# MLP in fp16 pieces: transfers in the order of the source, and what moves with them

## The chip, the cores and the metric

The kernel runs on one core of a Trainium2 chip. The metric is the device time of one execution in microseconds (us). Five engines work side by side, each through its own queue in order: TensorE (PE, matmuls and transposes), VectorE (DVE), ScalarE (ACT), GpSimd (POOL) and SyncE (SP), which here only issues transfers. A transfer is issued by SP, and lands some us later; the waits of SP's queue hold everything that is issued behind them.

## The reference, cut to what matters

One layer of an encoder on 1024 rows of width 1024 in float32: attention, an output projection with a residual, an MLP of width 4096 with a residual, and a last norm. The change touches the second norm and the MLP.

```python
def rms_norm(x, g):
    y = xf * lax.rsqrt(jnp.mean(xf * xf, axis=-1, keepdims=True) + EPS)
    return (y * g.astype(jnp.float32)).astype(x.dtype)
...
        h = h + jnp.einsum('bsm,md->bsd', y, w_out[layer])
        n2 = rms_norm(h, norm2_g[layer])
        u = jnp.square(jax.nn.relu(jnp.einsum('bsd,df->bsf', n2, w_ff1[layer])))
        h = h + jnp.einsum('bsf,fd->bsd', u, w_ff2[layer])
    return rms_norm(h, final_norm_g)
```

## The kernel before

**Pieces.** The MLP computes float32 products in float16: each operand is scaled by a power of two, taken from the largest magnitude in it, and split into a high and a low half; `mm3` makes three matmuls of it (high x high, high x low, low x high). `split` makes the halves: ACT writes the high one (L1357), and DVE (L1361) or POOL (L1359) the low one. A 2 x 2 block product is made of seven products of sums of blocks instead of eight; a product is 24 matmuls of 128 x 512. Its number p says which sums it takes, and the products of a group come in the order 1, 5, 6, 3, 7, 2, 4 (the last group of phase 2 in another).

**Phase 1** makes u from the normed rows: eight groups n, one for each 512 columns of w_ff1, with seven products each; "(n, p)" is one of them. Its weight tiles are w1 (four to a group), their sums T and their halves W; PE adds into PSUM tiles f1. Between products the maximum over each result is kept (topf), ACT takes relu and square, and after p = 4 DVE adds the pieces (k and v tiles, L1421 to L1427). The seven results of a group are stored to DRAM as ud, one transfer each (`put`, L1440).

**Phase 2** makes the output from u and w_ff2: four groups g of two parts n, seven products p for each part, first both parts of one p, then of the next: V0_1, V1_1, V0_5, V1_5 and so on. Its u tiles are loaded from ud one product's operand at a time (`load2u`, L1492), its weights w2 eight tiles to a group (`load2w`, L1498); U and V are the halves of both and Z the sums of weights. PE adds into f2 tiles (chains a, b and c, two banks each); when both parts of a product are through, DVE adds the bank to the output's accumulators C (`add_up`, L1637), which frees the bank for a later product. The operands of a product are made two products ahead (`prepare2`).

**Scales.** A scale needs the maximum over all partitions. `see` takes the maximum of a tile (tops), `gather` (L1163) that of its columns (top), and then it has to reach all partitions. In phase 1, and for the first group of phase 2, PE transposes it (`spread`, all_w and all_u). In phase 2 it goes through DRAM: `write` (L1170) stores top, `read` (L1174) loads it back to all partitions. Then `bits` (L1178) reduces it to topall and a few operations on single columns make the scale (up, uup) and what undoes it (down, udown). A row of n2 is multiplied by xup, a power of two from the gain's maximum, beside its rstd (L1219).

**What sets the order.** Each engine's instructions are put in a fixed order ahead of time by a planner that estimates when operands and buffers will be there; the loop over products gives it the work, and a manual dependency can force an order (the class `InOrder` chains what is issued through it, as the source has it). Before, SP's transfers are left to that planner.

## Time and profile before

| | us |
|---|---|
| three runs, median (lowest to highest) | 1085.91 (1085.35 to 1087.11) |
| the profiled execution | 1085.46 |
| its span | 1083.7 |
| PE busy | 1013.8 |
| DVE busy | 790.1 |
| ACT busy | 652.2 |
| POOL busy | 402.2 |

The span counts from the first to the last instruction. The mean granted clock of PE over it is 0.975. A busy time counts an engine's instructions, not its waits; the list of waits adds an engine's idle time up by what ended it, as total, number of times and longest one. In the groups of instructions, and in the timeline, numbers of buffers are left out (w2_4_00 is w), and the name is what is written, then what is read. A timeline row has the start, the length, the engine, the line and the operation, and in brackets the idle time before it.

### The profile page before, as it was taken

The page shows a single profiled execution, that of the slowest core. Times are in us where ns is not written, and L with a number is a line of the kernel's source. Part 1 is how long each engine was busy: PE and PEld are TensorE (multiplying, and loading weights), DVE is VectorE, ACT ScalarE, POOL GpSimd, SP SyncE. Part 2 cuts the span into 40 slices and gives each one's busy share as a digit, 9 for nine tenths or more (in the row PEclk, how much of TensorE's full clock was granted, in tenths as well). Part 3 has the DMA queues.
Part 4 walks back from the last instruction along what each step waited for, and adds up shares of the span by engine and source line. Part 5 has one row for each costly group of instructions (what it writes and reads, how often), then busy time and mean ns, then how long its engine had stood idle before and what let it go on. Part 6 is the DMA issues. An engine that isn't in the chain of part 4 may idle for free.

```text
span 1083.7 us, 13981 instructions
## 1 busy us (share of the span) xinstructions
PE 1013.8 (94%) x4815; PEld 594.1 (55%) x4815; DVE 790.1 (73%) x1299; ACT 652.2 (60%) x1033; POOL 402.2 (37%) x327
## 2 busy tenths in 40 slices
PE   9999999999979999899899899899898899799997
PEld 7888877777656777444344344344343344244443
DVE  6477787867667377978556566569988699588886
ACT  8676767666767656865466376368364444365446
POOL 0467674254434723041534434343131023035113
PEclk9999999999989999999999999999899899899999
DMA  9943628999999933133434344278897254251004
GB/s 361 249 130 97 165 78 192 201 214 218 242 216 250 279 139 135 59 117 139 153 119 174 136 143 167 98 268 309 260 333 271 80 175 155 80 194 39 1 1 155
DMA packets 142726, 184.04 MB, mean 170 GB/s; under 512 B 78656, under 2 KB 96576, under 8 KB 142656
## 3 DMA queue, kind: packets, MB, share of 16 engines
q1 hardware_dynamic: 142512, 182.89, 56.7%
q8 instruction: 38, 0.62, 0.3%
q14 instruction: 32, 0.26, 0.1%
q10 hardware_dynamic: 144, 0.26, 0.1%
HBM read 103.43 MB, written 42.99 MB: 135 GB/s over the span
## 4 chain that ended last, share of the span: by engine, by line
PE 28%; DVE 19%; DMA 9%; ACT 9%; issue 6%; POOL 2%; SPq 0%; DVEq 0%; ACTq 0%; POOLq 0%
PE f L169 9%; PE f_a L169 6%; DMA w<-in_w_ff_dram 4%; PE op_A L169 4%; DVE tops_w L1158 3%; PE f_c L169 3%; DVE V L1361 3%; ACT w L1324 2%; PE op_B L169 2%; PE f_b L169 2%; DVE C L1637 2%; DMA u<-ud 2%; DVE T L1331 2%; DVE Z L1331 1%; DMA top<-top_w 1%
## 5 line engine op out<-in xcount | busy, mean ns | idle before, releaser
L169 PE MATMUL f<-X,W 128*128 128x512 f16 x1344 | 299.3, 385 | 3.5 <-POOL W L1359 2.8
L169 PEld LDWEIGHTS <-U 128*128 128x128 f16 x1356 | 133.8, 99 | 191.2 <-issue 28.1
L169 PEld LDWEIGHTS <-W 128*128 128x128 f16 x1344 | 133.0, 99 | 166.0 <-issue 9.8
L169 PE MATMUL f_a<-V,U 128*128 128x512 f16 x756 | 171.6, 388 | 18.6 <-DVE C L1637 13.6
L1359 POOL TENSOR_TENSOR U<-u,U 128x1024 f16<-128x1024 f32 x32 | 76.9, 2411 | 237.8 <-ACT U L1357 216.4
L1359 POOL TENSOR_TENSOR W<-T,W 128x1024 f16<-128x1024 f32 x29 | 65.4, 2266 | 104.3 <-ACT W L1357 99.7
L1158 DVE TENSOR_REDUCE tops_w<-w 128x1 f32<-128x1024 f32 x64 | 76.2, 1213 | 33.6 <-DMA w<-in_w_ff_dram 33.6
L169 PE MATMUL f_c<-V,U 128*128 128x512 f16 x384 | 85.9, 384 | 5.4 <-DVE up L1140 4.2
L1359 POOL TENSOR_TENSOR W<-w,W 128x1024 f16<-128x1024 f32 x23 | 54.0, 2347 | 93.3 <-ACT W L1357 63.6
L1355 ACT ACTIVATE u<-u,uup 128x1024 f32<-128x1024 f32 x32 | 36.4, 1143 | 64.5 <-DMA u<-ud 64.4
L169 PE MATMUL op_A<-w_o,y 128*128 128x512 f32 x192 | 58.2, 431 | 8.1 <-DVE ts_vB L430 5.2
L617 ACT ACTIVATE P_B<-P_B,nm_B 128x640 f32<-128x640 f32 (+2 forms) x64 | 44.2, 690 | 29.6 <-DVE nm_B L614 14.4
L862 DVE SCALAR_TENSOR_TENSOR H_B<-P_B,rc_B,H_B 128x640 f16<-128x640 f32 (+2 forms) x64 | 51.0, 825 | 10.4 <-ACT H_B L857 10.0
L169 PE MATMUL ip_qB<-nT,w_qB 128*128 128x512 f32 x192 | 53.8, 406 | 1.1 <-DVE t_kB L404 1.0
L1403 ACT ACTIVATE k<-f 128x1024 f32<-128x1024 f32 x24 | 24.4, 1018 | 49.6 <-PE f L169 49.5
L1413 DVE CUSTOM_DVE_ANT_0 k<-f,k 128x1024 f32<-128x1024 f32 x24 | 29.2, 1219 | 34.4 <-PE f L169 34.2
L169 PE MATMUL ip_kB<-nT,w_kB 128*128 128x512 f32 x192 | 53.7, 405 | 0.0
L1414 ACT ACTIVATE k<-k,down 128x1024 f32<-128x1024 f32 x24 | 27.4, 1142 | 41.1 <-DVE topf L1413 41.0
L1357 ACT ACTIVATE V<-Z,up 128x1024 f16<-128x1024 f32 x32 | 36.5, 1140 | 25.3 <-DVE Z L1331 22.9
L169 PE MATMUL ip_vB<-nT,w_vB 128*128 128x512 f32 x192 | 51.2, 400 | 0.0
L1357 ACT ACTIVATE U<-u,uup 128x1024 f16<-128x1024 f32 x24 | 27.4, 1141 | 38.8 <-DMA u<-ud 15.5
L169 PE MATMUL ip_qA<-nT,w_qA 128*128 128x512 f32 x192 | 50.2, 395 | 0.3 <-DVE VA L175 0.3
(273 smaller groups left out, 2035.5 us busy)
## 6 DMA issues: line engine op xcount, KB each, us to landing
w<-in_w_ff_dram SPq DMA_DIRECT2D x64, 512.0 KB, 5.8
u<-ud SPq DMA_DIRECT2D x56, 512.0 KB, 5.3
ud<-k SPq DMA_DIRECT2D x48, 512.0 KB, 2.6
KkB<-t_kB SPq DMA_DIRECT2D x32, 256.0 KB, 5.1
xr<-in_x_dram SPq DMA_DIRECT2D x8, 512.0 KB, 8.6
st_o<-in_w_out_dram SPq DMA_DIRECT2D x8, 512.0 KB, 4.9
h<-in_x_dram SPq DMA_DIRECT2D x8, 512.0 KB, 4.8
hB<-h SPq DMA_DIRECT2D x8, 512.0 KB, 2.6
```

Of the source, the lines that this page charges most:

```text
L169: pe(nc.tensor.matmul(*args, **kw))
L617: nc.scalar.activation(pr, pr, AF.Exp, bias=nm, scale=-1.0, accum_out=sm)
L862: nc.vector.scalar_tensor_tensor(lo, q, rc, hi, ALU.mult, ALU.subtract)
L1158: nc.vector.tensor_reduce(self.column(), flat(src), mybir.AxisListType.X, ALU.max, apply_absolute_value=True)
L1331: engine.tensor_tensor(t, a, b, op)
L1355: nc.scalar.activation(full, full, AF.Copy, scale=up)
L1357: nc.scalar.activation(w[0], full, AF.Copy, scale=1.0 if up is None else up)
L1359: engine.tensor_tensor(w[1], full, w[0], ALU.subtract)
L1361: engine.scalar_tensor_tensor(w[1], full, up, w[0], ALU.mult, ALU.subtract)
L1403: nc.scalar.activation(kept[p], ps, AF.Copy)
L1413: dve.tensor_tensor_reduce(v, ps, v, 1.0, 0.0, ALU.add, ALU.max, top)
L1414: nc.scalar.activation(v, v, AF.Relu, scale=down1[n])
```

## The change

- **Transfers in the source's order.** From the start of the MLP's loop all its transfers go through `InOrder`, so that SP issues them as the program's loops have them.
- **Stores one product later.** `put` only notes a store; the notes are issued when the next product has been written. What is left after group 7 is issued at the end of phase 1, ahead of phase 2's loop.
- **u scales.** The transpose of a pair of groups' u maximum comes at (n, 3) instead of (n, 5).
- **Weights.** All four w1 tiles come from the same pool of pages. The w2 tiles of the next group are loaded two at a time at four steps, and their maxima are taken three steps after the load. top is written at step 8 instead of 9 and still read at step 10. The last u scale is written, read and made at steps 1, 3 and 6 instead of 1, 2 and 5, and the last C is loaded at step 9 instead of 5.
- **u in staging tiles.** u tiles go in turn to two small pools of three tiles each instead of to pages, and are loaded four products ahead instead of three.
- **Rows.** The power of two goes into the scale and the epsilon of the norm's own rstd (`rstd` with `scale` and `eps`), and the eight multiplications of r by xup go.

```diff
@@
-    def rstd(ss, n, width, name, r=None, then=None):
+    def rstd(ss, n, width, name, r=None, then=None, scale=None, eps=None):
...
-        nc.scalar.activation(u, ss, AF.Sqrt, bias=eps4, scale=1.0 / (4 * n))
+        scale = 1.0 / (4 * n) if scale is None else scale
+        nc.scalar.activation(u, ss, AF.Sqrt, bias=eps4 if eps is None else eps, scale=scale)
...
-        r = rstd(ss, D, 1, f"n2_{tb}")
-        nc.vector.tensor_tensor(r, r, xup, ALU.mult)
+        r = rstd(ss, D, 1, f"n2_{tb}", scale=xscale, eps=xeps)
@@
-                w1s[n, kh, j] = (page1 if j or (n, kh) == (1, 1) else stage)([P, 4, 2 * P], f"w1_{n}_{kh}{j}")
-                load(w1s[n, kh, j], src.rearrange("(k p) c -> p k c", p=P))
+                w1s[n, kh, j] = page1([P, 4, 2 * P], f"w1_{n}_{kh}{j}")
+                queue[0].dma_start(w1s[n, kh, j], src.rearrange("(k p) c -> p k c", p=P))
@@
+        while stores:
+            stores.pop(0)()
         kept = saved.setdefault(n, {})
@@
     def put(n, p, v):
-        nc.sync.dma_start(flat(ud[n][p - 1]), v)
+        stores.append(lambda: queue[0].dma_start(flat(ud[n][p - 1]), v))
@@
     def load2u(n, p):
-        u2s[n, p] = page([P, 2, HALF], f"u{n}_{p}", F32)
-        nc.sync.dma_start(u2s[n, p], ud[n][p - 1])
+        if len(u2s_made) % 2 == 0 or len(u2s_made) == 1:
+            u2s[n, p] = stage([P, 2, HALF], f"u{n}_{p}")
+        else:
+            u2s[n, p] = main.tile([P, 2, HALF], F32, tag="tst", bufs=TST, name=f"u{n}_{p}")
+        u2s_made.append((n, p))
+        queue[0].dma_start(u2s[n, p], ud[n][p - 1])
@@
+    queue[0] = InOrder(nc.sync)
     for at, (n, p) in enumerate(order1):
...
-        if p == 5 and n and n % GQ == 0:
+        if p == 3 and n and n % GQ == 0:
             scale_of_u(n // GQ - 1)
...
+    while stores:
+        stores.pop(0)()
     mp_.close()
@@
         if g + 1 < NQ // GQ:
-            if step in range(8):
-                load2w(*blocks2(g + 1)[step])
-            if step in range(2, 10):
-                see2(g + 1, blocks2(g + 1)[step - 2 :][:1])
-            if step in (9, 10):
-                (top2[g + 1].write if step == 9 else top2[g + 1].read)()
+            loads = (0, 1, 2, 3) if g else (1, 2, 4, 5)
+            if step in loads:
+                for tile2 in blocks2(g + 1)[2 * loads.index(step) :][:2]:
+                    load2w(*tile2)
+            if step - 3 in loads:
+                see2(g + 1, blocks2(g + 1)[2 * loads.index(step - 3) :][:2])
+            if step in (8, 10):
+                (top2[g + 1].write if step == 8 else top2[g + 1].read)()
@@
-        if g == 0 and step in (1, 2, 5):
+        if g == 0 and step in (1, 3, 6):
...
-        if at in (0, 1, 3, 5):
-            load_acc(*into[{0: 1, 1: 5, 3: 6, 5: 4}[at]])
+        if at in (0, 1, 3, 9):
+            load_acc(*into[{0: 1, 1: 5, 3: 6, 9: 4}[at]])
```

The planner's fixed orders move with it. Line numbers of the changed kernel are 3 to 19 higher here, and what goes through `InOrder` shows that class's line (L150). Three places follow; a row has the line, the operation, what it writes and reads, and the shape, and the last number of a name is the buffer's.

**DVE at group 7 of phase 1**, about the scale of w2's first group (tops_w2_0, top_w2_0, topall_w2_0). The ISA rows are the addition with a maximum at the end of product (7, 3). Before:

```order
L1158 TENSOR_REDUCE tops_w2_0_6854<-w2_1_10_6822 128x1
L1423 TENSOR_TENSOR v6_6761<-k6_1_6538,v6_6761 128x1024
L1331 TENSOR_TENSOR T7_4_6946<-w1_7_10_6504,T7_6_6784 128x1024
L1163 TENSOR_REDUCE top_w2_0_6894<-tops_w2_0_6854 128x1
L1425 TENSOR_TENSOR k6_1_6538<-k6_5_6568,k6_1_6538 128x1024
L1427 TENSOR_TENSOR k6_6_6610<-k6_6_6610,k6_1_6538 128x1024
L1413 ISA k7_6_6888,topf_7_6929<-f1_7_5_6827,k7_6_6888 128x1024
L1413 ISA topf_7_6929 128x1
L1178 TENSOR_REDUCE topall_w2_0_6936<-all_w2_0_6934 128x1
```

and now:

```order
L1161 TENSOR_REDUCE tops_w2_0_6849<-w2_1_00_6811 128x1
L1161 TENSOR_REDUCE tops_w2_0_6849<-w2_1_01_6813 128x1
L1161 TENSOR_REDUCE tops_w2_0_6849<-w2_1_11_6815 128x1
L1419 ISA k7_6_6883,topf_7_6924<-f1_7_5_6822,k7_6_6883 128x1024
L1419 ISA topf_7_6924 128x1
L1161 TENSOR_REDUCE tops_w2_0_6849<-w2_1_10_6817 128x1
L1166 TENSOR_REDUCE top_w2_0_6889<-tops_w2_0_6849 128x1
L1181 TENSOR_REDUCE topall_w2_0_6930<-all_w2_0_6928 128x1
```

The pass over (7, 3) now stands ahead of the last tile's maximum and of top_w2_0; before, it stood behind both. On PE the transpose that reads top_w2_0 stands right behind (7, 3) both times.

**SP at the boundary of the phases.** ud7 are the stores of group 7, u0 and u1 loads of phase 2, C the accumulators. Before:

```order
L1440 DMA ud6_3_152<-k6_6_6610 128x1024
L1492 DMA u1_5_7071<-ud1_5_119 128x1024
L1498 DMA w2_2_00_7073<-in_w_ff2_dram 128x2x512
L1605 DMA C000_7083<-hB0_88 128x2x512
L1605 DMA C001_7085<-hB1_89 128x2x512
L1492 DMA u0_6_7115<-ud0_6_113 128x1024
L1498 DMA w2_2_01_7117<-in_w_ff2_dram 128x2x512
L1440 DMA ud7_2_158<-k7_6_6888 128x1024
L1605 DMA C110_7128<-hB2_90 128x2x512
L1605 DMA C111_7130<-hB3_91 128x2x512
```

and now:

```order
L150 DMA u0_5_6895<-ud0_5_112 128x1024
L150 DMA ud7_2_158<-k7_6_6883 128x1024
L150 DMA ud7_4_160<-k7_5_6847 128x1024
L150 DMA ud7_1_157<-k7_1_6809 128x1024
L150 DMA ud7_5_161<-k7_5_6847 128x1024
L150 DMA ud7_7_163<-v7_7041 128x1024
L150 DMA ud7_6_162<-k7_1_6809 128x1024
L150 DMA ud7_3_159<-k7_6_6883 128x1024
L150 DMA u1_5_7066<-ud1_5_119 128x1024
L150 DMA u0_6_7068<-ud0_6_113 128x1024
L150 DMA C000_7078<-hB0_88 128x2x512
L150 DMA C001_7080<-hB1_89 128x2x512
```

The store of k7_6 after its last addition (ud7_3) is now ahead of u1_5 and of all that phase 2 loads after it; before, u1_5 and the first C were issued ahead of every store of group 7.

**DVE in phase 2**, about the scale that comes back from DRAM (topall_w2_2; scales of group 2). Before, late in group 0:

```order
L1637 SCALAR_TENSOR_TENSOR C000_7083<-f2_0_b_0_7491,down2_0_6943,C000_7083 128x1024
L1163 TENSOR_REDUCE top_w2_2_7974<-tops_w2_2_7712 128x1
L1637 SCALAR_TENSOR_TENSOR C001_7085<-f2_0_b_1_7492,down2_0_6943,C001_7085 128x1024
L1331 TENSOR_TENSOR Z3_5_7674<-w2_3_01_7279,w2_3_00_7243 128x1024
L1361 SCALAR_TENSOR_TENSOR U3_5_7676<-u3_5_7632,uup_1_6035,U3_5_7676 128x1024
L1178 TENSOR_REDUCE topall_w2_2_8088<-all_w2_2_8012 128x1
L1331 TENSOR_TENSOR Z2_6_7714<-w2_2_11_7160,Z2_5_7636 128x1024
L1133 TENSOR_SCALAR topall_w2_2_8088<-topall_w2_2_8088 128x1
L1361 SCALAR_TENSOR_TENSOR V3_5_7679<-Z3_5_7674,up2_1_7561,V3_5_7679 128x1024
```

and now, in the middle of group 1:

```order
L1652 SCALAR_TENSOR_TENSOR C111_7127<-f2_1_c_1_7724,down2_1_7560,C111_7127 128x1024
L1365 SCALAR_TENSOR_TENSOR U2_7_7872<-u2_7_7792,uup_1_6099,U2_7_7872 128x1024
L1365 SCALAR_TENSOR_TENSOR V2_7_7875<-Z2_7_7870,up2_1_7558,V2_7_7875 128x1024
L1335 TENSOR_TENSOR Z3_7_7904<-w2_3_11_7277,w2_3_01_7239 128x1024
L1365 SCALAR_TENSOR_TENSOR U3_7_7906<-u3_7_7827,uup_1_6099,U3_7_7906 128x1024
L1652 SCALAR_TENSOR_TENSOR C010_7205<-f2_1_a_0_7643,down2_1_7560,C010_7205 128x1024
L1181 TENSOR_REDUCE topall_w2_2_8085<-all_w2_2_8009 128x1
L1365 SCALAR_TENSOR_TENSOR V3_7_7909<-Z3_7_7904,up2_1_7558,V3_7_7909 128x1024
L1652 SCALAR_TENSOR_TENSOR C011_7207<-f2_1_a_1_7644,down2_1_7560,C011_7207 128x1024
```

Before, it stood ahead of the splits of V3_5, the second p of group 1, and of C100, the last addition of group 0; now it stands behind the addition of f2_1_a, which holds product V3_6.

More of the change, by code (lines that the diff above doesn't have):

```diff
@@ L38 @@
 AHEAD2 = 2
-LOAD2 = 3
+LOAD2 = 4
 LOOK_AHEAD = 2
@@ L51 @@
 V_UP = 13
-PAD = 88
+PAD = 80
 X_UP, W_UP, U_UP = 7, 12, 11
@@ L183, in rstd @@
         q = small.tile([P, width], F32, tag=f"rq{width}", bufs=2, name=f"q_{name}")
-        nc.scalar.activation(u, ss, AF.Sqrt, bias=eps4, scale=1.0 / (4 * n))
+        scale = 1.0 / (4 * n) if scale is None else scale
+        nc.scalar.activation(u, ss, AF.Sqrt, bias=eps4 if eps is None else eps, scale=scale)
         if then is not None:
             nc.scalar.activation(warm, u[:, :1], then, scale=0.0)
-        nc.vector.tensor_scalar(w, ss, 1.0 / (4 * n), EPS / 4, ALU.mult, ALU.add)
+        nc.vector.tensor_scalar(w, ss, scale, EPS / 4 if eps is None else eps, ALU.mult, ALU.add)
         nc.vector.reciprocal(q, u)
@@ L1126, in tst @@
         return main.tile(shape, F32, tag="tst", bufs=TST, name=name)
+    queue = [nc.sync]
     def page16(shape, name, alloc=None):
@@ L1169, in write @@
         def write(self):
-            nc.sync.dma_start(tops[self.slot].rearrange("a p -> p a"), self.top)
+            queue[0].dma_start(tops[self.slot].rearrange("a p -> p a"), self.top)
         def read(self):
             self.all = small.tile([P, P], F32, tag="all", bufs=1, name=f"all_{self.name}")
-            nc.sync.dma_start(self.all, tops[self.slot][0].partition_broadcast(P))
+            queue[0].dma_start(self.all, tops[self.slot][0].partition_broadcast(P))
         def bits(self, least=-90):
@@ L1185 @@
     nc.sync.dma_start(g2b, norm2_g.partition_broadcast(P))
-    xup, xdown = scale_tile("xup", "", 1), scale_tile("xdown", "", 1)
+    xdown, xscale, xeps = (scale_tile(t, "", 1) for t in ("xdown", "xscale", "xeps"))
     def scale_of_x():
@@ L1190, in scale_of_x @@
         nc.vector.tensor_reduce(top, g2b, mybir.AxisListType.X, ALU.max, apply_absolute_value=True)
-        e = bits_of(top, "x")
-        power(xup, e, -1.0, 254 + X_UP)
+        e = bits_of(top, "x", -40)
         power(xdown, e, 1.0, -X_UP)
+        nc.vector.tensor_tensor(xscale, xdown, xdown, ALU.mult)
+        nc.vector.tensor_scalar(xeps, xscale, EPS / 4, None, ALU.mult)
+        nc.vector.tensor_scalar(xscale, xscale, 1.0 / (4 * D), None, ALU.mult)
     opb = {}
@@ L1437 @@
     topf, topu = {}, {}
+    stores = []
     def put(n, p, v):
-        nc.sync.dma_start(flat(ud[n][p - 1]), v)
+        stores.append(lambda: queue[0].dma_start(flat(ud[n][p - 1]), v))
     saved = {}
@@ L1484 @@
         steps()
-    u2s, w2s = {}, {}
+    u2s, w2s, u2s_made = {}, {}, []
     def load2u(n, p):
-        u2s[n, p] = page([P, 2, HALF], f"u{n}_{p}", F32)
-        nc.sync.dma_start(u2s[n, p], ud[n][p - 1])
+        if len(u2s_made) % 2 == 0 or len(u2s_made) == 1:
[4 more added lines that the diff above has]
+        queue[0].dma_start(u2s[n, p], ud[n][p - 1])
     def load2w(n, i, j):
@@ L1497, in load2w @@
             src = w_ff2[n * HALF + i * 2 * P : n * HALF + (i + 1) * 2 * P, j * HALF : (j + 1) * HALF]
-            nc.sync.dma_start(w2s[n, i, j], src.rearrange("(a p) c -> p a c", p=P))
+            queue[0].dma_start(w2s[n, i, j], src.rearrange("(a p) c -> p a c", p=P))
         return w2s[n, i, j]
@@ L1585 @@
             if p == 6:
-                for i in range(LOAD2):
+                for i in range(LOAD2 - 1):
                     fetch2(i)
@@ L1604, in load_acc @@
             acc[i, j, n] = page([P, 2, HALF], f"C{i}{j}{n}", F32)
-            nc.sync.dma_start(acc[i, j, n], hB[2 * i + n][:, :, j * HALF : (j + 1) * HALF])
+            queue[0].dma_start(acc[i, j, n], hB[2 * i + n][:, :, j * HALF : (j + 1) * HALF])
     gfb = fp.tile([P, D], F32, tag="gb", name="gfb")
@@ L1705 @@
     for at, (g, p, n) in enumerate(order2[:-GQ]):
+        if at == 0:
+            fetch2(LOAD2 - 1)
         fetch2(at + LOAD2)
@@ L1719 @@
             nc.vector.reciprocal(up, down)
-        if g == 0 and step in (1, 2, 5):
+        if g == 0 and step in (1, 3, 6):
             last = NQ // GQ - 1
-            {1: topu[last].write, 2: topu[last].read, 5: lambda: scale_of_u(last, False)}[step]()
+            {1: topu[last].write, 3: topu[last].read, 6: lambda: scale_of_u(last, False)}[step]()
         prepare2(at + AHEAD2)
-        if at in (0, 1, 3, 5):
-            load_acc(*into[{0: 1, 1: 5, 3: 6, 5: 4}[at]])
+        if at in (0, 1, 3, 9):
+            load_acc(*into[{0: 1, 1: 5, 3: 6, 9: 4}[at]])
         if at == 6:
-            nc.sync.dma_start(gfb, final_g.partition_broadcast(P))
+            queue[0].dma_start(gfb, final_g.partition_broadcast(P))
         if product2(g, p, n):
```

## The prediction

> **What bounds the kernel now.** I read the busy times first, then what the matmul engine (PE) waited for, then its timeline around each wait, then the engine that released it.
>
> ```profile
> PE 1013.8 (94%) x4815; PEld 594.1 (55%) x4815; DVE 790.1 (73%) x1299; ACT 652.2 (60%) x1033; POOL 402.2 (37%) x327
> 728.63 8.37 PE L169 MATMUL f<-X,W 128*128 128x512 f16 x38
> ```
>
> PE is busy 1013.8 of a span of 1083.7 us, so the gain to be had is in its idle 70 us and in matmuls that run slowly behind idle time. The second row gives the undisturbed pace: 38 matmuls in 8.37 us, the last one lasting about 0.38, so (8.37 - 0.38)/37 = 0.216 us each and 24 x 0.216 = 5.18 us a product. Next, PE's waits in the MLP: phase 1 (450 to 752 us), then phase 2 (752 to 1067).
>
> ```profile
> PE all_u L172 <- DVE top_w L1163: 5.7, 2, 2.8
> PE all_u L172 <- DVE top_u L1163: 4.0, 1, 4.0
> PE f L169 <- POOL W L1359: 2.8, 3, 1.2
> ...
> PE f_a L169 <- DVE C L1637: 13.6, 5, 7.0
> PE f_a L169 <- DVE top_w L1163: 4.7, 1, 4.7
> PE f_c L169 <- DVE up L1140: 4.2, 1, 4.2
> PE f_b L169 <- DVE C L1637: 1.3, 2, 0.7
> PE f_c L169 <- DVE C L1637: 1.1, 1, 1.1
> ```
>
> Every row but the third names DVE. The timeline of PE shows what each long wait costs in all (the idle time stands in brackets):
>
> ```profile
> 530.05 7.68 PE L169 MATMUL f<-X,W 128*128 128x512 f16 x27
> 608.53 0.32 PE L172 MATMUL all_u<-ident,top_u 128*128 128x128 f32 x1 [2.83 <-DVE top_w L1163]
> 608.69 8.54 PE L169 MATMUL f<-X,W 128*128 128x512 f16 x31
> 688.54 8.75 PE L169 MATMUL f<-X,W 128*128 128x512 f16 x33
> 779.07 9.10 PE L169 MATMUL f_a<-V,U 128*128 128x512 f16 x31 [5.25 <-DVE C L1637]
> 840.80 9.39 PE L169 MATMUL f_a<-V,U 128*128 128x512 f16 x33 [4.65 <-DVE top_w L1163]
> 857.63 8.75 PE L169 MATMUL f_c<-V,U 128*128 128x512 f16 x32 [4.21 <-DVE up L1140]
> 931.19 5.98 PE L169 MATMUL f_a<-V,U 128*128 128x512 f16 x21 [6.97 <-DVE C L1637]
> 516.96 1.25 PE L169 MATMUL f<-X,W 128*128 128x512 f16 x5 [1.19 <-POOL W L1359]
> ```
>
> At 0.216 us the 31 matmuls behind the wait at 608 would take 30 x 0.216 + 0.38 = 6.86 us; they took 8.54. So a wait of 2.83 us costs another 1.7, and the same sum gives 1.7, 1.5, 2.2, 2.1, 1.7 and 1.3 for the other rows in order. The 1.19 us wait is followed by matmuls at full pace (4 x 0.216 + 0.38 = 1.24). I therefore price a wait of 2.8 us or more at itself plus 1.7, and one of about 2 us or less at itself.
>
> The Trainium skill (TensorE: Matmul & The Clock Gate, "What's actually happening") has the clock fall only after an idle window of about 3.4 us, counted by a free-running window; the 2.83 us rows disagree, or the window is shorter here, so the measurement decides. By that rule the one new wait of 2.8 us below would cost 2.8 instead of 4.5 and the forecast would be 1.7 us lower.
>
> The two worst waits of phase 2 are one cause, the round trip of a scale through DRAM, seen on DVE and on SP:
>
> ```profile
> 842.96 1.28 DVE L1361 SCALAR_TENSOR_TENSOR U<-u,uup,U 128x1024 f16<-128x1024 f32 x1
> 853.55 0.29 DVE L1178 TENSOR_REDUCE topall_w<-all_w 128x1 f32<-128x128 f32 x1 [9.31 <-DMA all_w<-top]
> 929.47 0.29 DVE L1178 TENSOR_REDUCE topall_w<-all_w 128x1 f32<-128x128 f32 x1 [8.92 <-DMA all_w<-top]
> 840.75 0.32 SPq L1170 DMA_DIRECT2D top<-top_w  x1
> 847.80 0.32 SPq L1174 DMA_DIRECT2D all_w<-top  x1
> ```
>
> DVE runs in order: it stands 9.31 and 8.92 us at topall_w while adds (C) that free PSUM banks and splits of U and V are queued behind it. The write took 847.80 - 840.75 = 7.05 us and the read 5.7 (to 853.5), about 12.8 in all.
>
> **The change, part by part.**
>
> *u scales in phase 1 (removed waits).* The three all_u transposes stand two products (10.4 us) later on PE, and top_u moves ahead of the k and v additions on DVE. The waits were 2.8, 2.8 and 4.0, so they fit inside 10.4 with 6 us to spare. Gain 4.5 + 4.5 + 5.5 = 14.5 us; the bounds are 14.5 and, if one of the three stayed, 9.
>
> *POOL W at the head of a phase 1 group.* DVE's weight maxima no longer stand ahead of that work, so I take 2.0 of the 2.8 us; bounds 0 and 2.8.
>
> *Norm and out-projection.* Eight small multiplies leave the row scale, and a tops_w reduction no longer stands before rB.
>
> ```profile
> 387.93 1.21 DVE L1158 TENSOR_REDUCE tops_w<-w 128x1 f32<-128x1024 f32 x1
> 395.30 1.63 PE L169 MATMUL op_B<-w_o,y 128*128 128x512 f32 x6 [1.97 <-DVE q_n L188]
> ```
>
> The wait that this feeds is 1.97 us, and another DVE chain comes next, so I take 1.0; bounds 0 and 2.0.
>
> *The new wait at all_w2_0.* PE still asks for the scale of group 0 right after product (7,3). Before, top_w was long done. Now the stores of group 6 go ahead of the second four weight tiles, and on DVE the k7_6 maximum, which needs the end of that same product, stands ahead of the last tops_w2.
>
> ```profile
> 735.07 0.15 DVE L1163 TENSOR_REDUCE top_w<-tops_w 128x1 f32<-128x8 f32 x1
> 736.83 0.27 PE L172 MATMUL all_w<-ident,top_w 128*128 128x128 f32 x1
> 739.45 1.21 DVE L1413 CUSTOM_DVE_ANT_0 k<-f,k 128x1024 f32<-128x1024 f32 x1
> ```
>
> So after (7,3) come 1.21 (k7_6), 1.21 (tops), 0.15 (top) and about 0.2 for two hand-overs: 2.8 us, and 1.7 of slow matmuls. Loss 4.5; bounds 2.8 and 7 (the last weight tile later than product (7,3)).
>
> *Head of phase 2.* In the source's order u1_5 follows all seven stores of group 7, so nothing of phase 2 is loaded between u0_5 and the end of k7. Call the end of phase 1's last matmul 0. The rows for the chain and for the DVE work behind it (phase 2's groups of instructions; the last row is the landing of the four loads of u between 735 and 760):
>
> ```profile
> 754.28 1.10 ACT L1410 ACTIVATE v<-f,down 128x1024 f32<-128x1024 f32 x1
> L1361 DVE SCALAR_TENSOR_TENSOR V<-Z,up,V 128x1024 f16<-128x1024 f32 x32 | 42.9, 1340 | 10.0 <-ACT V L1357 7.7 <-issue 2.1
> L1361 DVE SCALAR_TENSOR_TENSOR V<-w,up,V 128x1024 f16<-128x1024 f32 x22 | 42.7, 1947 | 3.6 <-ACT V L1357 3.5
> L1637 DVE SCALAR_TENSOR_TENSOR C<-f_a,down,C 128x1024 f32<-128x1024 f32 x30 | 37.5, 1276 | 0.0
> L1361 DVE SCALAR_TENSOR_TENSOR U<-u,uup,U 128x1024 f16<-128x1024 f32 x23 | 29.4, 1278 | 2.6 <-ACT U L1357 2.4
> L1331 DVE TENSOR_TENSOR Z<-w,w 128x1024 f32<-128x1024 f32 x14 | 18.9, 1355 | 2.8 <-PE f_c L169 2.7
> L1427 DVE TENSOR_TENSOR k<-k,k x8: 2872/3022/3141, 503.3 to 771.8; 128x1024 f32<-128x1024 f32 x8
> 771.46 5.19 POOL L1359 TENSOR_TENSOR U<-u,U 128x1024 f16<-128x1024 f32 x2 [25.25 <-ACT U L1357]
> DMA to landing us min/median/max: 4.2/8.7/10.1
> ```
>
> v 1.1, then on DVE five passes of 1.21 (the maximum of v and four adds, as long as k7_6's pass above) and three small ones of 0.15: k7_6 is done at 7.8 and its store issued at 8.2. u1_5 behind it lands in 4.2 (the least of the loads of u around 740; the longer ones had a full queue ahead, which this one has not): 12.4. ACT's U 1.1, DVE's U 1.28, Z 1.21 and V 1.28: V1_5 at 17.3, where PE wants it at 3 x 5.18 = 15.5. That is a wait of 1.8. The last k pass needs weighing: L1427 took 2.9 to 3.1 us all eight times, and the last began at 771.8, inside POOL's 771.46 to 776.65. In the change POOL has no u loaded at that point, so I take 1.2; with 3.0 V1_5 would be 1.8 later. The Trainium skill (GPSIMD Engine Reference, "1. Specifications") says that GpSimd's SBUF interfaces are shared with VectorE, in contention where a DVE instruction has two SBUF inputs; the row agrees, and by that rule too the pass would run at its short time. Bounds of this wait: 0 and 6 (3.0, a landing 1.1 longer, and 1.7 of slow matmuls).
>
> Behind it DVE is full. From V1_5 to V0_2, the first product of p = 2, its order holds 8 C, 4 U, 3 Z, 7 V (4 from Z, 3 from weights) and 8 maxima of 1.21: 10.2 + 5.1 + 4.1 + 5.4 + 5.8 + 9.7 = 40.3, less 0.07 x 30 since consecutive starts overlap: 38. V0_2 is ready at 55.5, PE wants it at 10 x 5.18 = 51.8. PE loses at least 3.7 by then, and since the waits do not fall one inside the other I take 7.0 for the whole group; bounds 2 and 14. Before, this stretch lost 7.5 (779) + 6.8 (840) + 2.1 in small waits (1.3 of f_b, the rest of f_a) = 16.4. The wait at 840 goes since up2_1 no longer stands behind eight late maxima: top13 is written at about 58, 12.8 later the scale is back at 71, V2_1 is ready at 74, wanted at 72.5 + 7 = 79.5. This is the tightest step, 5 us. Gain 9.4; bounds 2.4 and 14.4.
>
> *Groups 1 to 3.* The write now stands at step 8 and DVE's topall_w2_2 and _3 stand a dozen places later, behind adds of products V3_6 and V5_5 that end after the round trip's 12.8 us. So both waits of 9 us on DVE go, and with them 857 (4.2 + 1.7), 931 (7.0 + 1.3) and the 1.1 of f_c: 15.3. What is late next: w2_7's last pair is issued behind u5_3, which waits for POOL's split of U5_1, and its maxima stand ahead of the add C001 that frees V4_1's second bank, by my count 4 us early. I keep 2.0 for that. Gain 13.3; bounds 7 and 15.3. The staging tiles give a u load a way of six products, 31 us, against a round of 4.2 to 10.1 landing, 1.1 + 1.1 on ACT and at most 3.1 on POOL, 15.4 together, so they cost nothing; without that cover each of the 50 reloads would show with its 4.2 us at least.
>
> **Sum**, from the profiled execution's 1085.46 us (the median of the runs is 1085.91): -14.5 - 2.0 - 1.0 + 4.5 - 9.4 - 13.3 = -35.7, so 1049.8 us; I say 1050.
>
> **The rivals.** *DVE is the bound in group 0* and the late loads cost their upper bounds: 7 at all_w2_0, 6 at V1_5 with some 6 behind it, 4 at V4_1. That is 2.5 + 5 + 2 above the forecast, with a group that starts late: 1060. For it speaks that DVE is full there; against it, that half of that work was done before V0_6 in the old order too.
>
> *The boundary is cheap*: u1_5 and the maxima hide, no residue at V4_1: 1050 - 7 - 2 = 1041. For it speaks POOL's idleness, against it the count of DVE work.
>
> *Phase 2 does not gain* (the change does not do what it says there, because DVE's own work fills the time it no longer stands still): only the first four terms, 1085.5 - 13.0 = 1072.5. Against it:
>
> ```profile
> 942.00:1067.00 125.00, 124.22 (x576) 56.19 (x575) 105.57 (x101) 66.14 (x79) 38.37 (x18) 1.00 0.20 66
> ```
>
> Where no round trip is open, PE is busy 124.2 of 125 us with DVE at 105.6.
>
> *The ordered SP queue becomes the bound*: one transfer that waits holds all behind it, and every reload of a staging tile is late. Eight rounds of six tiles remain; a round of T us costs 8.3 x (T - 31.1). The change is slower once T passes 35.4; at 36 us it takes 1050 + 41 = 1091. It would need 20 us of standing on SP in each round (35.4 less the 15.4 above); the 7.05 us of the write is a third of that.
>
> **How the numbers follow.** Forecast 0.60, DVE-bound 0.18, cheap boundary 0.11, phase 2 without gain 0.05, SP-bound 0.06. A time within 0.2% of before (2.2 us, about what a measurement of this kernel can tell from no change) can only be part of the last, 0.02 of it; faster 0.94, slower 0.04. The range 1041 to 1066 holds the forecast with the bounds of its terms as far as they do not all fall one way, most of the DVE-bound case and the slower half of the cheap one; phase 2 without gain, the SP-bound case and those tails, about 0.2 together, are left out.
>
> **What would show it.** Right: no wait above 0.5 us before all_u; a wait of 2 to 4 us before all_w2_0 and one at V1_5, released by DVE; DVE's topall_w2_2 and _3 without idle time; PE busy in all but a few us from group 1 on. Wrong: waits of f_a on C in group 0 that sum to over 10 us, PE waits on DMA u or w, or DVE standing for maxima of w2_7 ahead of V4_1.

## The result, and the profile after

The changed kernel takes 1072.23 us (median of four runs, 1069.81 to 1075.31) against 1086.30 for the kernel before on the same chip: a ratio of 0.9872, 95% interval 0.9841 to 0.9904. It is faster by 14 us where 36 were forecast, and lies 6 us outside the range. Its profiled execution took 1074.07 us. The busy times:

```profile
span 1072.3 us, 13955 instructions
PE 1009.7 (94%) x4815; PEld 593.6 (55%) x4815; DVE 801.3 (75%) x1293; ACT 655.4 (61%) x1033; POOL 402.4 (38%) x327
```

PE's busy time fell by only 4 us, which is matmuls at full pace again behind waits that are gone; DVE's rose by 11. PE's waits in phase 1, and in phase 2, as before in the form total, times, longest:

```profile
PE all_w L172 <- DVE top_w L1166: 5.8, 1, 5.8
...
PE f L169 <- DVE topf L1419: 0.7, 1, 0.7
PE f L169 <- POOL W L1363: 0.2, 1, 0.2
...
PE f_a L169 <- DVE C L1652: 9.1, 7, 2.7
PE f_c L169 <- DVE C L1652: 5.5, 1, 5.5
PE f_c L169 <- DVE V L1365: 3.2, 2, 2.2
PE f_a L169 <- DVE V L1365: 2.9, 3, 1.9
```

Phase 1 has lost its three all_u rows and nearly all of the POOL row, and has one new wait, before all_w2_0. In phase 2 the waits for C are as long in sum as the forecast meant to end: 14.6 us here, 16.0 before. The waits for V are new, 7.9 us with three smaller ones: the operand itself is late.

Where the time went, stage by stage. The stages run from the start of one product's first matmul to that of another's on PE (W7_3 is product (7, 3) of phase 1, V2_1 product (2, 1) of phase 2); undisturbed, a group of phase 2 is 14 products or 72.5 us.

| stage, us | before | after | forecast change | measured change |
|---|---|---|---|---|
| attention, to the start of op_B | 374.87 | 378.63 | 0 | +3.8 |
| op_B to W0_1 (norm, out-projection) | 58.76 | 57.90 | -1.0 | -0.9 |
| W0_1 to W7_3 | 298.02 | 280.45 | -16.5 | -17.6 |
| W7_3 to V0_1 (all_w2_0) | 20.83 | 29.18 | +4.5 | +8.4 |
| V0_1 to V2_1 | 88.32 | 81.87 | | -6.5 |
| V2_1 to V4_1 | 80.67 | 87.87 | | +7.2 |
| V4_1 to V6_1 | 82.24 | 76.13 | | -6.1 |
| V0_1 to V6_4, all of phase 2 but its end | 314.34 | 309.26 | -22.7 | -5.1 |

The first row is no effect of the change: attention's code is the same, and in the traces of the experiments below op_B starts anywhere from 372.4 to 379.2. (Left out are the trace of the first experiment, taken at a granted clock of 0.791, and, in all ratios, the few executions that were far longer than the others of their kernel.) The shortfall lies in the last row, 17.6 us, and in all_w2_0, 3.9. What DVE waited for in phase 2, before (752 to 1067) and after (735 to 1056), shows the first:

```profile
DVE topall_w L1178 <- DMA all_w<-top: 18.2, 2, 9.3
DVE V L1361 <- ACT V L1357: 11.2, 8, 3.5
...
DVE U L1361 <- ACT U L1357: 2.4, 3, 1.5
```
```profile
DVE U L1365 <- ACT U L1361: 21.7, 6, 7.1
DVE V L1365 <- ACT V L1361: 18.3, 8, 9.1
```

Before, 18.2 us of DVE's waits were at topall_w, for the read of the scale. That wait is down to 1.2, but DVE stands 40.0 us behind ACT, 13.6 before. Its timeline has the three places:

```profile
820.75 2.26 DVE L1365 SCALAR_TENSOR_TENSOR V<-Z,up,V 128x1024 f16<-128x1024 f32 x1 [9.14 <-ACT V L1361]
823.01 0.29 DVE L1181 TENSOR_REDUCE topall_w<-all_w 128x1 f32<-128x128 f32 x1
...
878.63 1.28 DVE L1365 SCALAR_TENSOR_TENSOR U<-u,uup,U 128x1024 f16<-128x1024 f32 x1 [7.08 <-ACT U L1361]
...
950.04 1.28 DVE L1365 SCALAR_TENSOR_TENSOR U<-u,uup,U 128x1024 f16<-128x1024 f32 x1 [5.20 <-ACT U L1361]
```

The three waits are 21.4 us, in place of the 18.2 at topall_w. ACT in turn stood for a tile of u. SP's timeline around the first place, the one load of u issued at 806.14, and the issues of the stores with their median time to landing:

```profile
805.73 0.32 SPq L150 DMA_DIRECT2D top<-top_w  x1
806.14 0.38 SPq L150 DMA_DIRECT2D u<-ud  x1
...
813.81 0.33 SPq L150 DMA_DIRECT2D all_w<-top  x1
```
```profile
  ACT u L1359: 10.6, 1
...
DMA to landing us min/median/max: 11.2/11.2/11.2
```
```profile
top<-top_w SPq DMA_DIRECT2D x3, 0.5 KB, 8.1
```

The store of 0.5 KB takes 8.1 us, and the load of u right behind it 11.2: it lands 3.6 us after the store, about the 3.2 to 3.5 us that a load of u takes alone. The same holds for u3_4 (11.4) and u5_4 (7.5 behind a store that was half done). The DMA engines meanwhile (columns: stretch, us, busy PE, PEld, DVE, ACT, POOL, then clock, DMA share and GB/s):

```profile
805.70:814.00 8.30, 8.30 (x40) 3.75 (x39) 5.92 (x6) 1.15 (x1) 0.00 (x0) 1.00 0.75 35
814.00:823.00 9.00, 6.41 (x29) 2.74 (x28) 2.25 (x1) 3.40 (x4) 2.12 (x1) 1.00 0.91 300
```

They count as 75% busy while the store is open and move 35 GB/s; as soon as it has landed they move 300. The theory that the runs test is therefore that **the small store holds the loads behind it**, and that SP's new order puts a u that is due right there; the main rival is that DVE's own work is the bound in phase 2 and the waits only show it.

### The profile page after: what moved, and what is told of

Its sections match the earlier page's. It is cut to its first block, busy times and chain, and to the rows that moved or that the text cites. A ratio compares the mean times of both kernels' runs of the same rounds, so it can differ in the third digit from the quotient of the medians.

```text
span 1072.3 us, 13955 instructions
## 1 busy us (share of the span) xinstructions
PE 1009.7 (94%) x4815; PEld 593.6 (55%) x4815; DVE 801.3 (75%) x1293; ACT 655.4 (61%) x1033; POOL 402.4 (38%) x327
## 5 line engine op out<-in xcount | busy, mean ns | idle before, releaser
L169 PE MATMUL f_a<-V,U 128*128 128x512 f16 x756 | 168.2, 381 | 12.8 <-DVE C L1652 9.1
L1363 POOL TENSOR_TENSOR W<-T,W 128x1024 f16<-128x1024 f32 x29 | 63.2, 2180 | 96.6 <-ACT W L1361 96.6
L1361 ACT ACTIVATE W<-T 128x1024 f16<-128x1024 f32 x32 | 33.6, 1050 | 48.6 <-DVE T L1335 48.5
L863 DVE SCALAR_TENSOR_TENSOR H_B<-P_B,rc_B,H_B 128x640 f16<-128x640 f32 (+2 forms) x64 | 52.5, 848 | 10.5 <-ACT H_B L858 10.1
L1365 DVE SCALAR_TENSOR_TENSOR V<-Z,up,V 128x1024 f16<-128x1024 f32 x32 | 47.8, 1494 | 12.4 <-ACT V L1361 12.4
L169 PE MATMUL op_B<-w_o,y 128*128 128x512 f32 x192 | 48.4, 407 | 0.2 <-ACT o L1053 0.2
```

Source lines behind the costliest of these rows:

```text
L169: pe(nc.tensor.matmul(*args, **kw))
L863: nc.vector.scalar_tensor_tensor(lo, q, rc, hi, ALU.mult, ALU.subtract)
L1361: nc.scalar.activation(w[0], full, AF.Copy, scale=1.0 if up is None else up)
L1363: engine.tensor_tensor(w[1], full, w[0], ALU.subtract)
L1365: engine.scalar_tensor_tensor(w[1], full, up, w[0], ALU.mult, ALU.subtract)
```

## The experiments

Each ratio is to the kernel before on the same chip, whose median lay between 1084.69 and 1087.69. Each time is a median of four runs; the intervals are some 0.3% to either side. With each edit the planner may also place the work of DVE and ACT otherwise, so a difference of a few us is no proof of one cause.

**One line of the change alone.** The kernel before with u's scale two products later:

```diff
-        if p == 5 and n and n % GQ == 0:
+        if p == 3 and n and n % GQ == 0:
```

> The kernel before with one line of the change: the u scales are spread at (n, 3) instead of (n, 5). Theory A (phase 1's gain is the u scales, 14.5 us; phase 2's gain was eaten by new waits): 14 to 15 us faster than before, about 1072, as fast as the whole change. Rival B (phase 1's gain needs the ordered transfers too, since top_u would stand late on DVE without them): half of it or less, 1079 or more.

1072.31 us, 0.9854 (0.982 to 0.9887): as much as the whole change, and without ordered transfers. For its stages it was run a second time.

> The kernel before with one edit, u's scale worked out behind the product 3 instead of 5, once more for its trace: 1071-1074. The time from the first product's start to W7_3's falls by 14 to 15 us against before, as in the whole change, and phase 2 from the start of V0_1 to that of V6_4 takes what it took before, 314 us within 4. If phase 2 is shorter by more than 5 us, part of the change's phase 2 gain came from phase 1.

1072.35 us, 0.9882 (0.9854 to 0.9909). W0_1 to W7_3 takes 282.80, a gain of 15.2; phase 2 takes 315.0, as before. The POOL row stays, and about accounts for the 2.4 us between 282.80 and 280.45; which of the change's other edits ended it was not tried:

```profile
PE f L169 <- POOL W L1359: 2.7, 3, 1.2
```

So all the rest of the change adds up to nothing that these intervals can tell from zero. The runs that follow start from the changed kernel, except where another is named.

**The store behind the loads of its step** (at step 9, and last in it):

```diff
-            if step in (8, 10):
-                (top2[g + 1].write if step == 8 else top2[g + 1].read)()
+            if step == 10:
+                top2[g + 1].read()
...
         if at == 6:
             queue[0].dma_start(gfb, final_g.partition_broadcast(P))
+        if g + 1 < NQ // GQ and step == 9:
+            top2[g + 1].write()
         if product2(g, p, n):
```

> The changed kernel with the scale's store to DRAM issued one step later, behind the load of the next u (u1_4, u3_4, u5_4) and, in group 0, of two C tiles. Theory A (what is issued right behind the store lands some 7 us late, ACT stands for it in order and DVE for ACT): u3_4 and u5_4 land in 4 to 6 us instead of 11.4 and 7.5, DVE's waits of 7.1 and 5.2 us for ACT at U3_7 and U4_7 go, and the time falls by 5 to 8 us to about 1065; in group 0 DVE stands at the scale itself instead of at V1_4, so little is won there. Rival B (DVE is full, its waits are taken from slack): within 2 us of 1072.

1061.88 us, 0.9766 (0.9736 to 0.9796). The theory's direction, and some more than the 5 to 8 us expected: V2_1 to V6_1 takes 153.7 instead of 164.0.

**The store from ACT's queue**, and **a second store beside it**:

```diff
-            queue[0].dma_start(tops[self.slot].rearrange("a p -> p a"), self.top)
+            nc.scalar.dma_start(tops[self.slot].rearrange("a p -> p a"), self.top)
```
```diff
             queue[0].dma_start(tops[self.slot].rearrange("a p -> p a"), self.top)
+            queue[0].dma_start(tops[self.slot - NQ].rearrange("a p -> p a"), self.top)
```

> The changed kernel with the four stores of scales issued by ACT's queue instead of SP's. Theory A with the hold in SP's queue: u1_4, u3_4 and u5_4 land in 4 to 6 us, DVE's three waits of 9.1, 7.1 and 5.2 us shrink, 1058 to 1065. Theory A with the hold in the DMA engines themselves: the loads land as late as before, within 2 us of 1072. Rival B: within 2 us of 1072, with the loads landing early.

> The changed kernel with each of the four stores of scales issued twice, the second to a place that nothing reads. Theory A with the hold taken by the store's own passage: the loads behind land another 5 to 8 us later, DVE waits longer three times, 8 to 20 us slower than 1072. If the hold is a latency that two stores share, or if rival B holds: within 2 us of 1072.

1070.97 us (0.9847, 0.9822 to 0.9872) and 1069.6 us (0.9839, 0.9816 to 0.9862): neither moves much. A store issued by ACT at 855.4, with a load issued by SP at 857.1:

```profile
L1173 ACTq DMA_DIRECT2D top<-top_w x1: 326/326/326, 855.4 to 855.4; - x1
...
DMA to landing us min/median/max: 8.5/8.5/8.5
```
```profile
L150 SPq DMA_DIRECT2D u<-ud x1: 319/319/319, 857.1 to 857.1; - x1
...
DMA to landing us min/median/max: 10.4/10.4/10.4
```

The load of the other queue lands 3.5 us after the store: the hold is not SP's queue. The Trainium skill (DMA: Bandwidth & Descriptors, "Rules for kernel authors") says that the queues of SP and ACT run on the same 16 engines and interleave there; these rows agree. Two stores together:

```profile
L150 SPq DMA_DIRECT2D top<-top_w x2: 319/372/424, 802.2 to 802.5; - x2
...
DMA to landing us min/median/max: 8.4/8.4/8.5
```

256 pieces of four bytes land as soon as 128 do, and u1_4 behind them in 11.7 instead of 11.2. It is a delay that overlaps, not a passage of so many pieces one after the other.

**No trip at all, and a store of other pieces.** First, groups 1 to 3 take the scale of group 0's weights, and store and read are left out (the maxima are still made); then, on top of that, a store that nobody reads, of 128 pieces of 512 bytes:

```diff
-        up2[g] = power(scale_tile("up2", str(g), 2), e, -1.0, 254 + W_UP)
+            up2[g] = up2[0]
...
-            if step in (8, 10):
-                (top2[g + 1].write if step == 8 else top2[g + 1].read)()
```
```diff
+            if step == 8:
+                wide = small.tile([P, P], F32, tag="all", bufs=1, name=f"wide_{g}")
+                nc.vector.tensor_copy(wide, top2[g + 1].top.to_broadcast([P, P]))
+                queue[0].dma_start(wides[g], wide)
```

> The kernel after, without the store and the read of the weights' maxima of groups 1 to 3 of phase 2: their scale is that of group 0 (the maxima themselves are still worked out, some ten small instructions of DVE fewer). This leaves out the trip of three scales through DRAM. Theory (the store holds every load behind it by 7 to 8 us, and ACT and DVE then stand for u): DVE's stands of 9.1, 7.1 and 5.2 us behind ACT go, loads of u there land in less than 6 us instead of 11.2 to 11.4, PE loses less than 4 us instead of 18.6 between the starts of V2_1 and V6_4, and the time is 1053-1058. Rival (DVE's own work is the bound in groups 1 to 3, the stands only show that): no more than the 10 us that the store behind the loads gave, 1061-1066.

> As the run without the trip, with a store put back at the place of the old one that carries 128 pieces of 512 bytes rather than 128 of four (each maximum copied 128 times by DVE, about 0.3 us each time); nothing reads it. If the hold belongs to pieces of four bytes, the loads right behind land in less than 6 us, and the time is that of the run without the trip plus at most 2 us. If any store to DRAM holds what stands behind it, they land 10 us or more after their issue, and the time is 1066-1072.

1051.84 us (0.9687, 0.9658 to 0.9716) and 1059.31 us (0.9757, 0.9732 to 0.9782). Without the trip DVE's waits of 9.1 and 7.1 us are gone, and that of 5.2 is down to 3.0; of the 17.6 us missing in phase 2, 17.0 come back (292.27 from V0_1 to V6_4). The wide store and the load behind it:

```profile
L150 SPq DMA_DIRECT2D wide<-wide x1: 320/320/320, 806.0 to 806.0; - x1
...
DMA to landing us min/median/max: 1.5/1.5/1.5
```
```profile
L150 SPq DMA_DIRECT2D u<-ud x1: 383/383/383, 806.4 to 806.4; - x1
...
DMA to landing us min/median/max: 3.3/3.3/3.3
```

128 times the bytes land in 1.5 us instead of 8.1 and hold nothing. The time is 7.5 us worse than without the trip all the same, where at most 2 were expected. A second cost may be **SP itself**, which in the source's order cannot issue the loads behind the store until the store's maximum is there. SP's waits for it, in this run and in the next one:

```profile
SPq L150 <- DVE wide L1741: 37.9, 2, 21.8
```
```profile
SPq L150 <- DVE rows_w L1174: 40.3, 2, 24.6
```

But the next run stands as long, and its phase 2 is only 1.7 us above that without the trip, where this one's is 6.7 above. The planner also put DVE's work in another order here: the maxima of group 2's weights end at 854.2, and at 836.3 without the trip. So it is not shown that the 7.5 us are SP's standing. The Trainium skill (DMA: Bandwidth & Descriptors, "Specifications") says that below 512 bytes a transfer is a read, a modification and a write; the two stores lie on the two sides of that, and the next run shows that pieces under 512 bytes do not make the hold by themselves.

**The same bytes in four pieces.** DVE turns the column of 128 maxima into four rows of 32, so that the store has four pieces of 128 bytes:

```diff
-            queue[0].dma_start(tops[self.slot].rearrange("a p -> p a"), self.top)
+            rows = small.tile([P, 32], F32, tag="rows", bufs=1, name=f"rows_{self.name}")
+            nc.vector.transpose(rows, self.top.to_broadcast([P, 32]))
+            queue[0].dma_start(tops[self.slot].rearrange("a (p c) -> (a p) c", c=32), rows[0:P:32])
```

> The kernel after with this one edit: every scale's store in four pieces of 128 bytes. If what holds the loads is the 128 pieces of four bytes, the store lands in under 4 us, u1_4, u3_4 and u5_4 land in 3.3 to 6 us instead of 7.5 to 11.4, DVE's stands of 9.1, 7.1 and 5.2 us go, and the time is near that of the run with pieces of 512 bytes (1059.3) plus what the read of the scale costs: 1058-1062. If it is anything below 512 bytes a piece, or that a store stands ahead at all, nothing moves: 1069-1073.

1054.61 us, 0.9715 (0.9683 to 0.9747), 3.4 us below the range that was expected. The load right behind the store at 800.54 lands in 3.5 us:

```profile
L150 SPq DMA_DIRECT2D u<-ud x1: 382/382/382, 801.2 to 801.2; - x1
...
DMA to landing us min/median/max: 3.5/3.5/3.5
```

V0_1 to V6_4 is now 294.01.

**The weights ahead of the stores.** w2_1's four loads are issued ahead of the product at (7, 1), so ahead of group 6's stores:

```diff
+        if (n, p) == (NQ - 1, 1):
+            for tile2 in blocks2(0)[4:]:
+                load2w(*tile2)
...
-        if (n, p) in ((NQ - 2, 4), (NQ - 1, 1)):
-            for tile2 in blocks2(0)[(p == 1) * 4 :][:4]:
+        if (n, p) == (NQ - 2, 4):
+            for tile2 in blocks2(0)[:4]:
```

> The kernel after, with w2_1's four loads (half of group 0's weights of phase 2) issued before the product at (7,1), so ahead of group 6's four stores of u rather than behind them. Theory: PE's 5.8 us before all_w2_0 and the 2.2 us by which W7_7 ran long come from these four loads, which took 6.2 to 8.8 us behind the stores. Then the wait before all_w2_0 falls below 2 us and the time from the start of W7_3 to the start of V0_1 falls from 29.2 to 21-24 us: 1064-1068 us. Rival: DVE's row of maxima there is as late whatever the loads do, or group 0 gives the gain back because its own loads start no earlier: 1070-1073.

1066.33 us, 0.9826 (0.9801 to 0.985). The wait before all_w2_0 in the changed kernel, and here:

```profile
728.13 0.48 PE L172 MATMUL all_w<-ident,top_w 128*128 128x128 f32 x1 [5.80 <-DVE top_w L1166]
```
```profile
719.05 0.32 PE L172 MATMUL all_w<-ident,top_w 128*128 128x128 f32 x1 [0.38 <-DVE top_w L1166]
```

W7_3 to V0_1 falls by 7.8 to 21.42, but V0_1 to V2_1 rises by 4.3 to 86.18: part of the gain is lost again in group 0.

**The moves together, with the long and with the short store.** The store behind its step's loads, w2_1 ahead, and u1_5 fetched with the first three u (`range(LOAD2)` for `range(LOAD2 - 1)`); then the four pieces as well:

> The kernel after with three moves: the scale's store behind the step's loads, w2_1's loads ahead of group 6's stores, and the fourth load of u (u1_5) issued with the first three, ahead of group 7's last stores. Theory (each wait is that of a load behind a store): the sum of the single gains, 1061.9 less 4 to 8 for w2_1 less about 3 for u1_5's wait of 2.7 us, which is 1051-1055. Rival (what comes earlier at the head is lost again in group 0, where DVE's work is the bound): 1058-1062.

> The kernel of the three moves, with every scale's store turned on DVE into four pieces of 128 bytes (the column of 128 maxima becomes four rows of 32; one more small instruction of DVE for each of the four stores). Theory: the store then lands in under 4 us instead of 7.4 to 9.6, the one of u's maxima too (13.6 us there), the three stands before topall_w (10.9 us in all) fall below 4 us, and PE's 8.5 us of waits for C shrink with them: 1047-1051. Rival (PE waits there for DVE's own work on C, which does not move): 1053-1055.

1054.84 us (0.9716, 0.9687 to 0.9744) and **1038.56 us (0.9569, 0.9543 to 0.9596)**, the fastest of all and 8 us below what was expected. The rival of the second, that PE waits there for DVE's own work, falls: PE's waits for C go from 9.4 us to 3.2 and V0_1 to V6_4 takes 288.76. Group 0, 84.36 with the long store, takes 77.87: what comes earlier at the head is kept here.

The stretch from V2_1 to V6_1, 145 us at full pace, tells the two edits of the store apart:

| V2_1 to V6_1, us | long store | four pieces |
|---|---|---|
| store in its old place | 164.0 | 153.3 |
| behind its step's loads (with the two other moves) | 153.6 | 147.8 |

With the short store, which holds nothing, the moves still give 5.5 us there. That fits a cost of SP's standing, though the two moves at the head are in it too.

**Without the source's order.** One line of the change taken back, with the long store and with the short one:

```diff
-    queue[0] = InOrder(nc.sync)
```

> The kernel after without the ordering of SP's transfers (the scheduler places them, as in the kernel before; all other edits stay). If the hold belongs to the store and not to the order, the loads that the scheduler puts behind a store wait as long, at other places: 1069-1075. If the order itself costs (SP standing for a store's maxima with loads behind it; the runs without the store and with a wide one lie 7.5 us apart), it is 1062-1067. If the order was worth something, above 1077.

> The kernel after with the store in four pieces and without the ordering of SP's transfers. Each alone gave 17.0 to 17.6 us. One cause (the order harms only by putting loads behind the store): the two overlap but for the 7.3 us that the unordered transfers gained before V0_1, so 1046-1050. Two causes (the gains add): 1037-1041. If group 0 loses what the head gains, as it lost 6 us in the run without the order: 1052-1056.

1055.26 us (0.9716, 0.9688 to 0.9744), faster than any of the three cases had it, and 1053.97 us (0.9705, 0.9676 to 0.9735). Without the order 17.0 us come back, as many as with the short store, and both together give no more than either. That looks like one cause, but the stages say otherwise. With the short store, the end of the order gains 7.3 us from W7_3 to V0_1 (29.38 to 22.07: w2_1 no longer behind the stores) and loses 9.0 in group 0 (77.56 to 86.56).

Why group 0 is long then, the maxima of w2's tiles on DVE tell. Here is their row from 731 to 820 without the order, then the same with it:

```profile
L1161 DVE TENSOR_REDUCE tops_w<-w x24: 1168/1202/1210, 730.6 to 813.4; 128x1 f32<-128x1024 f32 x24
```
```profile
L1161 DVE TENSOR_REDUCE tops_w<-w x8: 1206/1208/1211, 764.1 to 790.8; 128x1 f32<-128x1024 f32 x8
```

With no order, the scheduler takes all 24 tiles of groups 1 to 3 into group 0, 16 maxima more than with it, 19 us of DVE's time where DVE is full. In the kernel before u's tiles filled the pages; that this is what holds the weights back, the next runs test.

**The change's phase 2 taken back.** The last run but without staging tiles (u in pages, and loaded three products ahead again), without pairs of weights, and without either:

```diff
-        if len(u2s_made) % 2 == 0 or len(u2s_made) == 1:
-            u2s[n, p] = stage([P, 2, HALF], f"u{n}_{p}")
-        else:
-            u2s[n, p] = main.tile([P, 2, HALF], F32, tag="tst", bufs=TST, name=f"u{n}_{p}")
-        u2s_made.append((n, p))
+        u2s[n, p] = page([P, 2, HALF], f"u{n}_{p}", F32)
```

> The run with four pieces and without the order (1053.97), with u loaded into pages three ahead, as before the change, in place of staging tiles four ahead. If the staging tiles are what costs (three and three buffers that come free only when ACT and the split are done with them, so loads start late), phase 2 falls from 301.4 to under 293 us and the time to 1043-1047. If they cost nothing: 1052-1056.

> The run with four pieces and without the order (1053.97), with the next group's weights loaded and measured one tile a step, as before the change. If the pairs are what costs (two transfers ahead of the u that is due, two maxima of DVE in one step), phase 2 falls from 301.4 to under 293 us and the time to 1043-1047. If they cost nothing: 1052-1056.

> The run with four pieces and without the order, with both taken back: weights one a step and u in pages. Left of the change are the norm's scales, the pages of the first weights, stores a product later and C's and u's scale steps. If the two are the whole cost, 1040-1045 and phase 2 within 3 us of 288.0. If the stores a product later or the moved steps carry part of it, above 1047.

1041.99 us (0.9587, 0.9559 to 0.9615), 1051.2 us (0.9675, 0.9651 to 0.9699) and 1041.02 us (0.9586, 0.9559 to 0.9613). The staging tiles with their longer way ahead cost 12 us, the pairs some 3 at most. With u in pages, 16 maxima instead of 24 come by 797:

```profile
L1161 DVE TENSOR_REDUCE tops_w<-w x16: 1176/1208/1215, 732.8 to 796.7; 128x1 f32<-128x1024 f32 x16
```

That fits a cost that is the room the staging tiles leave to the weights when nothing holds the order; the loads three instead of four ahead are in it too. With the order on, that was not tried.

**The kernel before with two edits**, u's scale and the four pieces, and the fastest kernel without the order:

> The kernel before with two edits, u's scale behind the product 3 and every scale's store in four pieces of 128 bytes; nothing else of the change. With the first edit alone it was 1072.35, and DVE stood 18.6 us before topall_w and 4.0 before topall_u. If these stands are most of what phase 2 lost there, they fall to some 7 us and the time to 1058-1064. If the change's other edits of phase 2 (pairs of weights, staging tiles, stores a product later) are needed for it, 1066-1072.

> The three moves and the four pieces, without the ordering of SP's transfers. If the order is of no use once the store is short, the time is within 3 us of that with it (1038.6): 1036-1041. If the scheduler's own order puts w2 or C ahead of a u that is due, group 0 takes over 81 us and the time is 1042-1048. If SP's standing was still a cost, 1031-1035.

1043.38 us (0.9608, 0.9584 to 0.9632), 15 us below what was expected, and 1046.77 us (0.9638, 0.9615 to 0.9661), with V0_1 to V2_1 at 86.27, as the second case had it. Two edits of the kernel before beat the change by 29 us; of the two, the four pieces are worth that much by themselves (1072.35 with the first edit only). From V2_1 to V6_4, 40 products that take 207.2 us at 5.18 each (first the changed kernel, then before with the two edits):

```profile
828.03:1055.43 227.40, 212.64 (x962) 94.28 (x961) 195.47 (x182) 119.09 (x130) 62.38 (x27) 0.98 0.41 126
```
```profile
813.93:1022.57 208.64, 207.52 (x961) 93.68 (x960) 180.43 (x171) 111.25 (x121) 57.69 (x26) 1.00 0.31 102
```

PE works through it with 1.1 us of idle time, at the full clock, with DVE at 180.4 us. The changed kernel has more DVE work there, 195.5, but that too is less than the 207.2 that PE needs: the sum of DVE's work is not the bound, though its order can be.

## Why the prediction was wrong, step by step

- **u scales: right.** No wait before all_u is left; the edit alone gains 15.2 us (14.5 forecast).
- **POOL W and the norm: right.** 2.4 and 0.9 (2.0 and 1.0).
- **The new wait at all_w2_0: right in kind, too small.** It is 5.8 us and 8.4 in all, not 2.8 and 4.5, and above the bound of 7. The case named for the upper bound held: w2_1's loads, behind group 6's stores, took 6.2 to 8.7 us to land, the last at 725.7, while product (7, 3) had ended at 722.3. DVE then stood for them:

```profile
721.61 2.58 DVE L1161 TENSOR_REDUCE tops_w<-w 128x1 f32<-128x1024 f32 x2 [1.87 <-DMA w<-in_w_ff_dram]
...
727.91 0.16 DVE L1166 TENSOR_REDUCE top_w<-tops_w 128x1 f32<-128x8 f32 x1
```

- **Head of phase 2: near, in part by luck.** Group 0 lost 9.4 us against the full pace (81.87 less 72.5); 7.0 was forecast, and before it lost 15.8. But with the short store it lost 5.1: 4.3 of the 9.4 go with the long store, behind which u1_4 came late, and the forecast did not have that.
- **Groups 1 to 3: the step that failed.** "Both waits of 9 us on DVE go" held for topall_w, and "I keep 2.0" did not: V2_1 to V6_1 lost 19.0 us against the full pace (164.0 less 145), 17.9 before. "What is late next" was sought among the weights; it was u. The step gave a load of u 4.2 to 10.1 us to land, from rows in which no scale's store stood ahead of it, and found 31 us of room. Behind the scale's store it took 11.2 and 11.4; and of the room little is left when SP, in order, issues that load only once the maximum of the store before it is there:

```profile
SPq L150 <- DVE top_w L1166: 32.2, 3, 18.1
```

The wait of 18.1 us is the one before the store at 805.73. What the runs showed in place of the step: without store and read phase 2 takes 292.3 instead of 309.3, and with the short store 294.0, so the short store gives back 15.3 us of the 17.6. Of the 19.0 us from V2_1 to V6_1 the short store ends 10.7, and the three moves with it 16.2. How much SP's standing costs by itself stays open: 1.7 us of phase 2 with the four pieces, 6.7 with the wide store. The row of the kernel before that could have warned was there: its trip through DRAM took 7.05 us for 0.5 KB. It was read as the price of a trip, not as a time in which nothing else lands.
- **The sum.** Of the 24.3 us between 1049.8 and the profiled 1074.07, phase 2 is 17.6, all_w2_0 3.9, attention 3.8; phase 1 gave 1.0 more than forecast.

Of the rivals, "phase 2 does not gain" has the right time (1072.5) and the wrong cause: it said that DVE's work fills the time, and with a short store group 2 of the changed kernel ran at full pace (72.52 from V4_1 to V6_1), group 1 not yet (80.81). "The ordered SP queue becomes the bound" had a part of the cause, at a price far too high: it asked for 20 us of standing in each round, and the runs with and without the order differ by 17.0 us in all. It set the 7.05 us of the write against those 20; SP stood for the maximum ahead of the write, 18.1 us. The signs to look for did their work in part: f_a's waits for C stayed at 9.1 us in all and no PE wait named a DMA, since ACT and DVE stood between u and PE; the sign that should have been there is DVE standing behind ACT.

## What to carry to other kernels

A transfer is not to be priced by itself alone: ask what is issued behind it, on any queue, and when that is due. A small store with one element a partition is best turned into a few long rows first, which here cost one short DVE instruction and was worth 17.6 us. And an edit that puts transfers in a fixed order moves each wait of the queue onto everything behind it, so before it goes in, look for the store whose data come late: here w2_1's loads behind group 6's stores, and u behind the scale's store, took back what phase 2 was to gain.
